# Hybrid decoder step, one core: plain products for four feed-forward pairs while the second token group's blocks are built, weight sums on DVE, and loads moved ahead

## The chip, the cores and the metric

The kernel runs on one core of a Trainium2 chip. The metric is device time in microseconds (us); lower is better. Five engines work side by side: PE (TensorE, matmuls and transposes), DVE (VectorE), ACT (ScalarE), POOL (GpSimd) and SP, which here only issues DMA transfers. Each engine goes through its own list of instructions in order; semaphores hold an instruction until what it reads is there or what it overwrites is free. PE writes to PSUM banks; everything else lies in SBUF or in device memory.

## The reference, cut to what matters

One decoder layer over 1024 prompt tokens and 32 sample tokens (1056 in all, width 1024): three branches, a gated merge, an output projection, and a gated feed-forward block (width 2816).

```python
merged = (sigmoid(g_a) * (y_a @ w_branch[:A_W]) + sigmoid(g_dn) * (y_dn @ w_branch[A_W:A_W + DN_V])
          + sigmoid(g_m) * (y_m @ w_branch[A_W + DN_V:]))
x = x + merged @ w_o
gate, up = split(rmsnorm(x, norm_ffn) @ w_up, 2)
x = x + (silu(gate) * up) @ w_down
y = rmsnorm(x, norm_final)
```

All values are 32-bit floats, and the result has to keep that precision.

## The kernel before, in words

**Three matmuls for one product.** PE multiplies in a shortened format, so each operand is split in a high and a low half (`split`: ACT casts the high half, DVE subtracts it from the source to get the low one), and a product is the sum of high*high, high*low and low*high. The tiles `pc` hold split weights, `raw` the weights as loaded, `bx` the split blocks of activations.

**Stages.** Up to about 1047 us the branches, ending with the last third of the merge (L273 to L275). Then the output projection `w_o` with the residual (`w_o_group`), the feed-forward up products with SiLU (`up_chunk`, to about 1661 us), the down products (L1246 to L1251, to about 1932 us), and the final norm.

**Token groups.** Group 0 holds the 128-token tiles 0, 2, 1, 3 and group 1 the tiles 4, 6, 5, 7 and the 32 sample tokens, called token 8. For each tile `w_o_group` makes two halves of 512 columns over eight blocks k of the inner dimension; DVE adds the residual out of PSUM (`tadd`), ACT squares and sums. After the second half `norm_t` (called once for each tile) reads the first half back from device memory, makes the factor `rstd` on DVE in twelve small steps, scales both halves of `xo` on DVE (L1206, L1207; `xo` has one buffer), PE transposes the eight blocks (L1213), and ACT writes them to `xf` with the gain (L1217). `combine` then makes differences of two tiles' blocks (on POOL for group 0, on DVE for group 1), and `put` splits each of the seven blocks 11, 21, 22, T1 to T4 into `bx`.

**Up products.** For each of 22 pairs f (128 columns of gate and 128 of up) and each group g, `up_chunk` uses the Strassen-Winograd form: seven block products of 12 matmuls each, 256 columns wide for group 0 and 272 for group 1, so 84 matmuls. The blocks of weights are seven pieces made by `up_pieces`: two DMA loads into `raw`, four sums or differences on POOL into a third `raw` tile and in place, and seven splits. Results come out of PSUM by DVE adds (L92), SiLU on ACT, two DVE products (L89), and two DMA stores to `dH`. The order `seq` is: group 0 of f = 0 to 6 (`NA` = 7), group 1 of f = 0 to 6, then both groups of f = 7 to 19 one after the other, and last (20,0), (21,0), (20,1), (21,1). Whoever changes f calls `up_pieces` anew, so it is called 31 times (62 loads). `raw` is a ring of 5 tiles and `pc` one of 8.

**Down products.** `h_load` reads `dH` back into `hr` (3 buffers) and splits it into `hx`, which lie in a pool `dp` that is opened once the up stage's pools are closed; `wd_load` loads the weights. At the end of each tile the residual is read as a whole row tile `x2` (512 KB).

**What sets the order.** A scheduler that goes by the priorities in `high_priority` (`AHEAD` = 3000, `CHAIN` = 4500) writes one list per engine. Pools decide when a load may start: a tile of a new pool waits until the tiles that lay there are done with.

Of the kernel before, what the change touches and what calls it, by code (L numbers as in the profile page):

```python
# [34 lines left out]
NA = 7  # L35
# [14 lines left out]
def kernel(  # L50
# [1101 lines left out]
    def sub_pool(name, side="left"):  # L1152
        c = ctx.enter_context(ExitStack())
        return c, c.enter_context(tc.tile_pool(name=name, bufs=1, side=side, reuse_waits="tile"))

    wctx, wp = sub_pool("wp")

    def raw_t():
        return wp.tile([P, 1024], F32, tag="raw", bufs=5, name=nm("raw"))

    def pc_t():
        return wp.tile([P, 1024], F32R, tag="pc", bufs=8, name=nm("pc"))
# [23 lines left out]
    def piece_tiles(pool_, g):  # L1186
        BX[g] = {p: pool_.tile([P, 2, 4, GN[g]], F32R, name=f"bx{g}{p}") for p in PIECES}
# [12 lines left out]
    def norm_t(i, x2, ss):  # L1200
        rows = tok[i][1]
        xo = wo.tile([P, D], F32, tag="xo", bufs=1, name=nm("xo"))
        nc.sync.dma_start(xo[:rows, 0:512], dX2[i][:rows, 0:512])
        add(V, ss[:rows, 0:1], ss[:rows, 0:1], ss[:rows, 1:2])
        r = rstd_of(ss[:rows, 0:1], 1, "rstd")
# [3 lines left out]
        for kh in range(2):  # L1209
            b = bank("d").rearrange("p (k c) -> p k c", k=4)  # L1210
            for kk in range(4):
                k = 4 * kh + kk
                T.transpose(b[:, kk, :rows], xo[:rows, k * P:(k + 1) * P], ident[:rows, :rows])  # L1213
            f = xf_t()
            for kk in range(4):
                k = 4 * kh + kk
                A.activation(f[:, kk, :rows], b[:, kk, :rows], AF.Copy, scale=gains[:, 2 * KT + k:2 * KT + k + 1])  # L1217
            out.append(f[:, :, :rows])
        return out

    def combine(g, cs, b11, b21, b12, b22):
        n = cs.stop - cs.start
        t1, t2 = (tt_t()[:, :, :n] for _ in range(2))
        E = V if g else G
        sub(E, t1, b12, b11)
        sub(E, b12, b22, b12)
        put(g, "11", cs, b11)
        put(g, "T1", cs, t1)
        sub(E, t2, b22, t1)
        put(g, "22", cs, b22)  # L1230
        put(g, "T3", cs, b12)
        put(g, "21", cs, b21)
        put(g, "T2", cs, t2)
        sub(E, b21, b21, t2)
# [20 lines left out]
    def tadd(b, i, x2, cs, lo):  # L1255
        rows = tok[i][1]
        add(V, x2[:rows, cs], b[:rows], x2[:rows, cs])
        if rows < P:
            A.copy(lo[:NS], b[NS:2 * NS])
            add(V, x2[:NS, cs], lo[:NS], x2[:NS, cs])  # L1260

    def w_o_group(g):
        ssq = {}
        for hf in range(2):
            cs = slice(hf * 512, hf * 512 + 512)
            ws = []
            for k2 in range(4):
                raw, hi, lo = raw_t(), pc_t(), pc_t()
                with tc.high_priority(offset=AHEAD):
                    nc.sync.dma_start(raw.rearrange("p (k c) -> p k c", k=2),  # L1270
                                      w_o[0, k2 * 256:(k2 + 1) * 256, cs].rearrange("(k p) c -> p k c", p=P))
                    split(hi, lo, raw)
                ws.append([a.rearrange("p (k c) -> p k c", k=2) for a in (hi, lo)])
            held = {}
            for i in groups[g]:
                t0, rows = tok[i]
                with tc.high_priority(offset=300):
                    x2 = x2_load(i, cs)
                b = bank("b")
                for k in range(KT):  # L1280
                    hi, lo = ws[k // 2]
                    x = X[k]
                    tmm(b, i, hi[:, k % 2], lo[:, k % 2], x[:, 0, t0:t0 + rows], x[:, 1, t0:t0 + rows], xs[:, k],
                        k == 0, k == KT - 1)
                pri = ExitStack()
                if hf == 1:
                    pri.enter_context(tc.high_priority(offset=CHAIN))
                tadd(b, i, x2, slice(0, 512), tt_t().rearrange("p k c -> p (k c)") if rows < P else None)
                if hf == 0:
                    ssq[i] = wo.tile([P, 2], F32, tag="ssq", bufs=5, name=nm("ssq"))  # L1290
                A.activation(bank("d")[:rows], x2[:rows], AF.Square, accum_out=ssq[i][:rows, hf:hf + 1])
                nc.sync.dma_start(dX2[i][:rows, cs], x2[:rows])
# [245 lines left out]
```

## Time and profile before

| | |
|---|---|
| time, median of 3 runs (lowest, highest) | 1943.93 us (1940.45, 1944.67) |
| the profiled execution, its own time | 1943.94 us |
| its span | 1941.8 us |
| PE busy | 1866.9 us (96%) |
| PE weight load busy | 1727.6 us (89%) |
| DVE busy | 1116.3 us (57%) |
| ACT busy | 716.2 us (37%) |
| POOL busy | 330.7 us (17%) |
| TensorE clock granted, mean of the span | 0.982 |

The span is the profiled part of one execution, and its rows are in microseconds from the span's start. A matmul's busy time is longer than the distance to the next matmul, since matmuls overlap in the array; what one costs is the stretch divided by the count, in a stretch without idle time. The granted clock (PEclk) is 1.00 at 2.4 GHz and 0.50 at 1.2 GHz; a value between them is a stretch with some of both. A wait is shown as who waited, for which instruction of which engine.

### The profile page before, as it was taken

How to read it: one execution, taken by the hardware profiler on the slowest of the kernel's cores; microseconds unless marked ns; L12 is line 12 of the kernel's file. 1: busy time of each engine (PE TensorE's matmuls, PEld its weight loads, DVE VectorE, ACT ScalarE, POOL GpSimd, SP SyncE). 2: the span in 40 equal slices, each digit the busy share in tenths (PEclk: the TensorE clock that was granted, in tenths of full speed). 3: DMA queues.
4: the chain of work that ended last, by engine and by line, in shares of the span. 5: the costliest groups of instructions: out<-in, count | busy, mean ns of one | idle time of the engine just before them, and what ended most of it. 6: DMA issues, size and time to landing. Idle time of an engine off the chain costs nothing. (4 is left out here: it accounts for less than half of the span.)

```text
span 1941.8 us, 31597 instructions
## 1 busy us (share of the span) xinstructions
PE 1866.9 (96%) x12145; PEld 1727.6 (89%) x12145; DVE 1116.3 (57%) x2558; ACT 716.2 (37%) x1539; POOL 330.7 (17%) x366
## 2 busy tenths in 40 slices
PE   6999999999999999999998998789999999899997
PEld 6799998889999999999998878789999999787776
DVE  6666477545743466622147479989665658456224
ACT  5523463234323452222222355444332324344121
POOL 3100011011000012000023044534232323001000
PEclk9999999999999999999999998889999999999999
DMA  5122123331322334321344534324232233855311
GB/s 171 33 69 80 47 67 94 110 117 58 105 83 64 90 94 125 113 72 43 109 145 173 175 117 128 115 76 121 70 92 75 67 94 123 288 185 188 110 64 46
DMA packets 229746, 203.58 MB, mean 105 GB/s; under 512 B 21284, under 2 KB 188121, under 8 KB 229596
## 3 DMA queue, kind: packets, MB, share of 16 engines
q1 hardware_dynamic: 229596, 201.58, 33.6%
q8 instruction: 95, 1.56, 0.3%
q14 instruction: 55, 0.45, 0.1%
HBM read 163.41 MB, written 38.12 MB: 104 GB/s over the span
## 5 line engine op out<-in xcount | busy, mean ns | idle before, releaser
L273 PE MATMUL psb<-x,whi 128*128 128x384 f32 (+1 forms) x1272 | 418.3, 329 | 1.6 <-ACT whi L102 1.2
L275 PE MATMUL psb<-x,wlo 128*128 128x384 f32 (+1 forms) x1272 | 415.2, 328 | 0.5 <-DVE wlo L95 0.5
L274 PE MATMUL psb<-x,whi 128*128 128x384 f32 (+1 forms) x1272 | 415.2, 327 | 0.0
L95 DVE TENSOR_TENSOR pc<-raw,pc 128x512 fp32r<-128x512 f32 (+1 forms) x278 | 273.3, 990 | 137.3 <-ACT pc L102 131.5
L102 ACT CAST pc<-raw 128x512 fp32r<-128x512 f32 (+1 forms) x278 | 196.1, 716 | 263.5 <-PE psb L1368 121.1
L273 PEld LDWEIGHTS psb<-x,whi 128*128 128x128 f32 x1272 | 239.6, 188 | 5.3 <-issue 1.9
L275 PEld LDWEIGHTS psb<-x,wlo 128*128 128x128 f32 x1272 | 239.9, 189 | 3.5 <-DVE wlo L95 1.4
L274 PEld LDWEIGHTS psb<-x,whi 128*128 128x128 f32 x1272 | 239.8, 189 | 3.1 <-issue 2.0
L1366 PE MATMUL psb<-bx,pc 128*128 128x272 f32 (+1 forms) x528 | 154.5, 293 | 9.5 <-DVE ev L92 7.4
L95 POOL TENSOR_TENSOR raw<-raw,raw 128x512 f32<-128x512 f32 x93 | 143.5, 1556 | 75.5 <-DVE pc L95 53.2
L95 DVE TENSOR_TENSOR wlo<-raw,whi 128x1024 fp32r<-128x1024 f32 x73 | 90.6, 1241 | 110.9 <-ACT whi L102 107.3
L1367 PE MATMUL psb<-bx,pc 128*128 128x272 f32 (+1 forms) x528 | 153.8, 291 | 0.0
L1368 PE MATMUL psb<-bx,pc 128*128 128x272 f32 (+1 forms) x528 | 153.2, 291 | 0.4 <-DVE rstd L110 0.4
L1246 PE MATMUL psb<-pc,hx 128*128 128x512 f32 x344 | 136.8, 398 | 6.0 <-ACT hx L102 6.0
L92 DVE TENSOR_TENSOR ev<-psb,ev 128x256 f32<-128x256 f32 (+1 forms) x220 | 93.9, 427 | 78.7 <-PE psb L1368 67.2
L1247 PE MATMUL psb<-pc,hx 128*128 128x512 f32 x344 | 137.0, 398 | 0.0
L1248 PE MATMUL psb<-pc,hx 128*128 128x512 f32 x344 | 132.4, 397 | 0.0
L1366 PEld LDWEIGHTS psb<-bx,pc 128*128 128x128 f32 x528 | 103.3, 196 | 11.0 <-ACT pc L102 5.1
L102 ACT CAST whi<-raw 128x1024 fp32r<-128x1024 f32 x73 | 76.5, 1048 | 89.3 <-PE psb L274 71.4
L1366 PE MATMUL psb<-bx0T,pc 128*128 128x256 f32 x352 | 101.0, 287 | 6.1 <-DVE ev L92 6.0
L1368 PEld LDWEIGHTS psb<-bx,pc 128*128 128x128 f32 x528 | 103.2, 196 | 0.7 <-DVE rstd L110 0.7
L1367 PEld LDWEIGHTS psb<-bx,pc 128*128 128x128 f32 x528 | 103.6, 196 | 0.1
(496 smaller groups left out, 3970.0 us busy)
## 6 DMA issues: line engine op xcount, KB each, us to landing
raw<-in_w_ffn_up_dram SPq DMA_DIRECT2D x62, 512.0 KB, 4.6
raw<-in_w_in_dram SPq DMA_DIRECT2D x56, 512.0 KB, 3.9
raw<-in_w_ffn_down_dram SPq DMA_DIRECT2D x44, 512.0 KB, 3.4
raw<-in_w_o_dram SPq DMA_DIRECT2D x16, 512.0 KB, 8.1
raw<-in_w_branch_dram SPq DMA_DIRECT2D x12, 512.0 KB, 3.8
dH<-ev SPq DMA_DIRECT2D x44, 136.0 KB, 3.4
hr<-dH SPq DMA_DIRECT2D x22, 272.0 KB, 3.1
dH<-ev SPq DMA_DIRECT2D x44, 128.0 KB, 1.7
```

Of the source, the lines that this page charges most:

```text
L92: eng.tensor_tensor(out, a, b, op=ALU.add)
L95: eng.tensor_tensor(out, a, b, op=ALU.subtract)
L102: A.copy(hi, src)
L273: T.matmul(o, w_h, xh[k][:, cs], start=k == 0, stop=False)
L274: T.matmul(o, w_h, xl[k][:, cs], start=False, stop=False)
L275: T.matmul(o, w_l, xh[k][:, cs], start=False, stop=k == nk - 1)
L1246: T.matmul(b, xh, wh, start=first, stop=False)
L1247: T.matmul(b, xh, wl, start=False, stop=False)
L1248: T.matmul(b, xl, wh, start=False, stop=last)
L1366: T.matmul(b, w[:, 0, k], x[:, 0, k], start=start and k == 0, stop=False, skip_group_check=not start)
L1367: T.matmul(b, w[:, 0, k], x[:, 1, k], start=False, stop=False, skip_group_check=not start)
L1368: T.matmul(b, w[:, 1, k], x[:, 0, k], start=False, stop=k == 3, skip_group_check=not start)
```

## The change

**Plain products.** `NA` is 4. Group 0 of f = 0 to 3 is no longer made by `up_chunk` but by `up_plain`: two loads, two splits over all 1024 columns, and eight block products of 12 matmuls (96 instead of 84) on the blocks 11, T1, 22 and 21, with four DVE adds and products and no weight sums. Group 1 of f = 0 to 3 is made by `up_chunk` later: one each is put in behind f = 6, 10, 14 and 18 (`QOUT`). `up_pieces` is called 24 times (48 loads, and 8 loads for the plain products).

**Sums and differences on DVE.** The four sums of `up_pieces` and the differences of `combine` of both groups are made by DVE.

**Norms.** `norm_pair` makes `rstd` for two tiles at once; `xo` is scaled by ACT and has two buffers. Group 1 goes through as (8), (4, 6), (5, 7), and all its `w_o` products stand ahead of the up products.

**Pools.** `raw` and `pc` lie in two pools, the first of them there while the merge still runs, and `raw` has 4 tiles. The first two `w_o` loads of the first half (k = 0 to 3) are issued and split during the merge. `ev` has 8 + 8 buffers used in turn. A pool `hp` with 11 `hx` and the 3 `hr` is opened where the blocks of group 0 lay. The down stage's residual comes by halves (`xl`, 2 buffers, 256 KB). `norm_final`'s gain is loaded early in the up stage.

```diff
-NA = 7
+NA = 4
+QOUT = 4
...
+    wps = [sub_pool("wpa")[1]]
...
+    def raw_t():
+        return ring_t("raw", 4, 2, F32)
+
+    def pc_t():
+        return ring_t("pc", 8, 4, F32R)
...
+        if f2 >= 2:
+            w_o_pre.append(w_o_load(0, f2 - 2))
...
-    def raw_t():
-        return wp.tile([P, 1024], F32, tag="raw", bufs=5, name=nm("raw"))
...
-    def norm_t(i, x2, ss):
...
-        V.tensor_scalar(xo[:rows, 0:512], xo[:rows, 0:512], r[:rows], None, op0=ALU.mult)
-        V.tensor_scalar(xo[:rows, 512:], x2[:rows], r[:rows], None, op0=ALU.mult)
...
+    def norm_pair(pair, x2s, ssq):
...
+        with tc.high_priority(offset=CHAIN):
+            r = rstd_of(ss[:rows, :n], n, "rstd")
...
+            xo = wo.tile([P, D], F32, tag="xo", bufs=2, name=nm("xo"))
+            nc.sync.dma_start(xo[:rows, 0:512], dX2[i][:rows, 0:512])
+            A.activation(xo[:rows, 512:], x2s[i][:rows], AF.Copy, scale=r[:rows, j:j + 1])
+            A.activation(xo[:rows, 0:512], xo[:rows, 0:512], AF.Copy, scale=r[:rows, j:j + 1])
...
-        E = V if g else G
-        sub(E, t1, b12, b11)
-        sub(E, b12, b22, b12)
+        sub(V, t1, b12, b11)
...
+    for pair, out in w_o_group(1, ((8,), (4, 6), (5, 7))):
+        todo.append((pair, out))
...
+    def up_plain(f):
...
+            for c0 in (f * P, DFF + f * P):
                 raw, hi, lo = raw_t(), pc_t(), pc_t()
+                nc.sync.dma_start(raw.rearrange("p (k c) -> p k c", k=KT), w_ffn_up[0, :, c0:c0 + P].rearrange("(k p) c -> p k c", p=P))
+                split(hi, lo, raw)
...
+            prod(b1, w, 0, "11", True, True)
+            p1_, c2 = ev_t(256), ev_t(256)
+            A.copy(p1_, b1)
+            prod(b2, w, 0, "T1", True, False)
+            prod(b2, w, 4, "22", False, True)
+            add(V, c2, b2, p1_)
+            prod(b1, w, 4, "21", False, True)
...
-            add(G, s1, a21, a22)
-            sub(G, s2, s1, a11)
+            add(V, s1, a21, a22)
+            sub(V, s2, s1, a11)
             piece("11", a11)
-            sub(G, s3, a11, a21)
+            sub(V, s3, a11, a21)
...
-            sub(G, s4, a12, s2)
+            sub(V, s4, a12, s2)
             piece("S4", s4)
...
-    seq = [(f, g) for g in range(2) for f in range(NA)]
+    for f in range(NA):
+        up_plain(f)
...
     for f in range(NA, NF - 2):
         seq += [(f, 0), (f, 1)]
+        if late_b and (f - NA) % QOUT == 2:
+            seq.append((late_b.pop(0), 1))
...
+    hp = sub_pool("hp")[1]
     bctx.close()
-
     dctx, dp = sub_pool("dp")
...
-        raw = dp.tile([P, 544], F32, tag="hr", bufs=3, name=nm("hr"))[:, :n]
-        hx = dp.tile([P, 2, 544], F32R, tag="hx", bufs=24, name=nm("hx"))[:, :, :n]
+        raw = hp.tile([P, 544], F32, tag="hr", bufs=3, name=nm("hr"))[:, :n]
+        hx = hx_t()[:, :, :n]
...
-                    with tc.high_priority(offset=100):
-                        nc.sync.dma_start(x2[i][:rows], dX2[i][:rows])
...
+                xl = dp.tile([P, 512], F32, tag="xl", bufs=2, name=nm("xl"))
+                with tc.high_priority(offset=60):
+                    nc.sync.dma_start(xl[:rows], dX2[i][:rows, cs])
```

The lists of the engines show the change at three places. A row has the line, the operation, what is written and read, and the shape.

PE before, at the last transposes of group 1 (`xo` of tile 7, then of token 8), between the last product of group 0 of f = 6 and the first of group 1 of f = 0:

```order
L1368 MATMUL psb_1804_12799<-bx022_11058,pc_1800_12793 128x256
L1213 MATMUL psd_1643_11783<-ident_69,xo_1639_11763 128x128 x4
L1213 MATMUL psd_1645_11793<-ident_69,xo_1639_11763 128x128 x4
L1213 MATMUL psd_1655_11849<-ident_69,xo_1651_11829 128x32 x4
L1213 MATMUL psd_1657_11859<-ident_69,xo_1651_11829 128x32 x4
L1366 MATMUL psb_1822_12933<-bx111_11873,pc_1815_12910 128x272
L1367 MATMUL psb_1822_12933<-bx111_11873,pc_1815_12910 128x272
```

PE after, at the first transposes of the pair (5, 7), inside the plain products of f = 3:

```order
L1364 MATMUL psb_1709_12286<-bx021_10825,pc_1704_12275 128x256 x2
L1247 MATMUL psd_1643_11773<-ident_69,xo_1642_11769 128x128 x4
L1247 MATMUL psd_1645_11783<-ident_69,xo_1642_11769 128x128 x4
L1364 MATMUL psb_1709_12286<-bx021_10825,pc_1705_12276 128x256
L1364 MATMUL psb_1713_12340<-bx011_10824,pc_1707_12281 128x256 x2
L1364 MATMUL psb_1713_12340<-bx011_10824,pc_1708_12282 128x256
```

Between the last transposes and the first product that reads group 1 stood nothing; now the products of f = 3 that remain and those of (4,0) stand there, and token 8 comes first of its group instead of last.

DVE before, in the group 1 passes over f = 0 to 6 (`pc` is a split of a weight piece, `ev` a result out of PSUM):

```order
L95 TENSOR_TENSOR pc_13051<-raw_13044,pc_13051 128x512
L92 TENSOR_TENSOR ev_12963<-psb_12934,ev_12949 128x272
L95 TENSOR_TENSOR pc_13054<-raw_13042,pc_13054 128x512
L92 TENSOR_TENSOR ev_12977<-psb_12935,ev_12963 128x272
L92 TENSOR_TENSOR ev_12991<-psb_12936,ev_12977 128x272
L95 TENSOR_TENSOR pc_13057<-raw_13044,pc_13057 128x512
L95 TENSOR_TENSOR pc_13060<-raw_13040,pc_13060 128x512
```

DVE after, in the passes over both groups (`raw` is a sum or difference of weights):

```order
L93 TENSOR_TENSOR raw_13766<-raw_13764 128x512
L96 TENSOR_TENSOR raw_13766<-raw_13766,raw_13762 128x512
L96 TENSOR_TENSOR raw_13764<-raw_13762,raw_13764 128x512
L93 TENSOR_TENSOR ev_13592<-psb_13550,ev_13578 128x256
L96 TENSOR_TENSOR raw_13762<-raw_13762,raw_13766 128x512
L93 TENSOR_TENSOR ev_13606<-psb_13551,ev_13592 128x256
L93 TENSOR_TENSOR ev_13634<-psb_13550,ev_13578 128x256
L90 TENSOR_TENSOR ev_13620<-ev_13620,ev_13634 128x256
L93 TENSOR_TENSOR ev_13649<-psb_13551,ev_13578 128x256
L96 TENSOR_TENSOR pc_13773<-raw_13766,pc_13773 128x512
```

The four weight sums of the next f now stand in DVE's list between the results of the running one, ahead of the splits; before they had a list of their own on POOL.

SP before, at the end of the up stage (`dH` stores of the last pair, and the first loads of `hr`, `y` being the residual):

```order
L1396 DMA dH_10790<-ev_17547 128x272
L1444 DMA raw_17872<-in_w_ffn_down_dram 128x2x512
L1397 DMA dH_10790<-ev_17576 128x272
L1433 DMA hr_17638<-dH_10771 128x512
L1433 DMA hr_17655<-dH_10772 128x512
L1433 DMA hr_17678<-dH_10773 128x512
L1444 DMA raw_17912<-in_w_ffn_down_dram 128x2x512
L1417 DMA g_fin<-in_norm_final_dram 128x1024
L1444 DMA raw_17928<-in_w_ffn_down_dram 128x2x512
L1490 DMA y_17978<-dX_0_10760 128x1024
```

SP after, in front of the last two `dH` stores:

```order
L1506 DMA hr_17599<-dH_10793 128x512
L1517 DMA raw_17426<-in_w_ffn_down_dram 128x2x512
L1455 DMA dH_10804<-ev_17233 128x272
L1517 DMA raw_17536<-in_w_ffn_down_dram 128x2x512
L1506 DMA hr_17622<-dH_10794 128x512
L1506 DMA hr_17639<-dH_10795 128x512
L1456 DMA dH_10804<-ev_17262 128x272
L1517 DMA raw_17616<-in_w_ffn_down_dram 128x2x512
L1506 DMA hr_17662<-dH_10796 128x512
L1517 DMA raw_17576<-in_w_ffn_down_dram 128x2x512
L1506 DMA hr_17679<-dH_10797 128x512
L1455 DMA dH_10805<-ev_17370 128x272
```

Before, the first `hr` load came after the last `dH` store; now most of the first pass's `hr` loads stand ahead of it, between the stores.

## Rows read from the trace of the kernel before

**Rows 1.** The page, part 1: busy us (share of the span) and instructions.

```profile
span 1941.8 us, 31597 instructions
PE 1866.9 (96%) x12145; PEld 1727.6 (89%) x12145; DVE 1116.3 (57%) x2558; ACT 716.2 (37%) x1539; POOL 330.7 (17%) x366
```

**Rows 2.** Stretches: length; busy (count) PE, PEld, DVE, ACT, POOL; PEclk; DMA share; GB/s.

```profile
1040.00:1060.00 20.00, 13.42 (x68) 12.00 (x67) 16.28 (x29) 7.86 (x13) 0.71 (x3) 0.83 0.14 49
...
1160.00:1260.00 100.00, 84.67 (x608) 81.31 (x606) 97.62 (x177) 49.89 (x115) 50.33 (x33) 0.88 0.39 117
1260.00:1280.00 20.00, 9.78 (x59) 9.28 (x58) 11.97 (x39) 9.59 (x33) 0.72 (x1) 0.59 0.10 30
1280.00:1340.00 60.00, 60.00 (x481) 59.99 (x480) 57.82 (x77) 28.44 (x56) 34.34 (x23) 1.00 0.38 113
1340.00:1640.00 300.00, 300.00 (x2449) 299.87 (x2449) 190.81 (x320) 100.65 (x203) 96.43 (x65) 1.00 0.29 87
...
1660.00:1680.00 20.00, 15.28 (x57) 11.93 (x56) 8.68 (x12) 7.15 (x11) 0.00 (x0) 0.83 0.92 313
1680.00:1700.00 20.00, 18.70 (x81) 14.82 (x80) 8.90 (x12) 8.96 (x13) 0.00 (x0) 1.00 0.86 304
1720.00:1920.00 200.00, 200.00 (x861) 155.59 (x860) 74.82 (x133) 55.35 (x80) 7.49 (x21) 1.00 0.33 110
1920.00:1942.00 22.00, 12.02 (x52) 9.37 (x50) 16.09 (x74) 2.90 (x8) 0.00 (x0) 0.84 0.28 101
```

**Rows 3.** PE's waits from 1040 us on: total us, times, longest.

```profile
PE psb L1366 <- DVE ev L92: 13.4, 8, 3.7
PE psd L1213 <- DVE xo L1206: 10.4, 3, 8.9
PE psb L1246 <- ACT pc L102: 6.6, 1, 6.6
PE psb L1246 <- ACT hx L102: 6.0, 2, 4.7
```

**Rows 4.** PE in order of time: start, us, operation [idle before, releaser]; token 8's transposes.

```profile
1269.18 1.03 PE L1213 MATMUL psd<-ident,xo 32*128 32x32 f32 x8 [8.89 <-DVE xo L1206]
```

**Rows 5.** DVE's groups by form, 1160 to 1280 us: count, busy us, mean ns.

```profile
L95 DVE TENSOR_TENSOR pc<-raw,pc 128x512 fp32r<-128x512 f32 x57 | 50.9, 907 | 2.5 <-ACT pc L102 2.5
L92 DVE TENSOR_TENSOR ev<-psb,ev 128x256 f32<-128x256 f32 x35 | 14.4, 412 | 0.0
L98 DVE SCALAR_TENSOR_TENSOR rstd<-rstd,rstd 128x1 f32<-128x1 f32 x24 | 11.9, 495 | 0.0
...
L95 DVE TENSOR_TENSOR tt<-xf,xf 128x512 f32<-128x512 f32 x2 | 1.4, 692 | 1.1 <-ACT xf L1217 1.1
...
L98 DVE SCALAR_TENSOR_TENSOR rstd<-rstd,rstd 32x1 f32<-32x1 f32 x6 | 0.9, 147 | 0.2
```

**Rows 6.** DVE in order of time, 1300 to 1310 us: start, us, operation.

```profile
1301.59 0.68 DVE L95 TENSOR_TENSOR pc<-raw,pc 128x512 fp32r<-128x512 f32 x1
1302.19 0.43 DVE L92 TENSOR_TENSOR ev<-psb,ev 128x272 f32<-128x272 f32 x1
1302.54 2.56 DVE L95 TENSOR_TENSOR pc<-raw,pc 128x512 fp32r<-128x512 f32 x2
```

**Rows 7.** POOL in order of time, 1300 to 1310 us.

```profile
1303.26 1.29 POOL L92 TENSOR_TENSOR raw<-raw 128x512 f32<-128x512 f32 x1 [3.44 <-DVE pc L95]
```

**Rows 8.** DVE's groups by form, 1655 to 1700 us.

```profile
L95 DVE TENSOR_TENSOR pc<-raw,pc 128x1024 fp32r<-128x1024 f32 x9 | 10.9, 1225 | 7.3 <-ACT pc L102 3.8 <-DMA hr<-dH 2.0 <-PE psb L1368 1.5
L95 DVE TENSOR_TENSOR hx<-hr,hx 128x512 fp32r<-128x512 f32 x13 | 8.7, 690 | 16.1 <-ACT hx L102 16.1
```

**Rows 9.** SP's issues in order of time, 1652 to 1672 us.

```profile
1662.20 1.39 SPq L1433 DMA_DIRECT2D hr<-dH  x3
```

**Rows 10.** The page, part 6: DMA issues, count, KB each, median us to landing.

```profile
raw<-in_w_ffn_up_dram SPq DMA_DIRECT2D x62, 512.0 KB, 4.6
...
raw<-in_w_o_dram SPq DMA_DIRECT2D x16, 512.0 KB, 8.1
```

More of the change, by code (lines that the diff above doesn't have):

```diff
@@ L1265, in w_o_group @@
             cs = slice(hf * 512, hf * 512 + 512)
+            ws = [w_o_pre.pop(0) if w_o_pre else w_o_load(hf, k2) for k2 in range(4)]
+            for pair in pairs:
+                x2s = {}
+                for i in pair:
+                    t0, rows = tok[i]
+                    with tc.high_priority(offset=300):
+                        x2 = x2_load(i, cs)
+                    b = bank("b")
+                    for k in range(KT):
+                        hi, lo = ws[k // 2]
+                        x = X[k]
+                        tmm(b, i, hi[:, k % 2], lo[:, k % 2], x[:, 0, t0:t0 + rows], x[:, 1, t0:t0 + rows], xs[:, k],
+                            k == 0, k == KT - 1)
+                    pri = ExitStack()
+                    if hf == 1:
+                        pri.enter_context(tc.high_priority(offset=2 * CHAIN))
+                    tadd(b, i, x2, x2, tt_t().rearrange("p k c -> p (k c)") if rows < P else None)
+                    if hf == 0:
+                        ssq[i] = wo.tile([P, 2], F32, tag="ssq", bufs=5, name=nm("ssq"))
+                    A.activation(bank("d")[:rows], x2[:rows], AF.Square, accum_out=ssq[i][:rows, hf:hf + 1])
+                    nc.sync.dma_start(dX2[i][:rows, cs], x2[:rows])
+                    x2s[i] = x2
+                    pri.close()
+                if hf == 1:
+                    with tc.high_priority(offset=CHAIN):
+                        out = norm_pair(pair, x2s, ssq)
+                    yield pair, out
@@ new lines, in build_pair @@
+    def build_pair(g, pair, out):
+        with tc.high_priority(offset=CHAIN):
+            if pair[0] < 8:
+                c = (pair[0] - 4 * g) * P
+                lo_, hi_ = out
+                combine(g, slice(c, c + P), lo_[0], lo_[1], hi_[0], hi_[1])
+            else:
+                s0, s1 = out[0]
+                combine(g, slice(256, 272), s0[:, :, :16], s1[:, :, :16], s0[:, :, 16:], s1[:, :, 16:])
+    piece_tiles(xa, 0)
+    for pair, out in w_o_group(0, ((0, 2), (1, 3))):
+        build_pair(0, pair, out)
@@ L1266, in w_o_group @@
+    todo = []
+    for pair, out in w_o_group(1, ((8,), (4, 6), (5, 7))):
+        todo.append((pair, out))
+    xctx.close()
+    g_fin = sub_pool("gf", "right")[1].tile([P, D], F32, name="g_fin")
+    bctx, xb = sub_pool("xb", "right")
+    piece_tiles(xb, 1)
+    for pair, out in todo:
+        build_pair(1, pair, out)
+    octx.close()
+    def up_plain(f):
+        with tc.high_priority(offset=AHEAD):
             ws = []
-            for k2 in range(4):
+            for c0 in (f * P, DFF + f * P):
@@ L1268, in w_o_group @@
                 raw, hi, lo = raw_t(), pc_t(), pc_t()
[L1269 to L1292, printed above, removed]
-                if hf == 1:
-                    held[i] = norm_t(i, x2, ssq[i])
-                pri.close()
-                if hf == 1:
-                    yield i, held
@@ new lines, in prod @@
+        def prod(b, w, k0, x, start, stop):
+            x = BX[0][x]
+            for k in range(4):
+                for wi, xi in ((0, 0), (0, 1), (1, 0)):
+                    T.matmul(b, w[wi][:, k0 + k], x[:, xi, k], start=start and k == wi == xi == 0, stop=stop and k == 3 and wi == 1,
+                             skip_group_check=True)
+        res = []
+        for w in ws:
+            b1, b2 = (bank("b")[:, :256] for _ in range(2))
+            prod(b1, w, 0, "11", True, True)
[5 more added lines that the diff above has]
+            prod(b1, w, 4, "21", False, True)
+            res.append((b1, c2))
@@ L1397, in up_chunk @@
         nc.sync.dma_start(dH[f][:, c0 + n:c0 + 2 * n], c12)
[L1399 removed]
+    for f in range(NA):
+        up_plain(f)
+    ectx, ev1 = sub_pool("ev1")
+    evs.append(ev1)
+    nev[0] = 0
+    seq = []
+    late_b = list(range(NA))
     for f in range(NA, NF - 2):
         seq += [(f, 0), (f, 1)]
+        if late_b and (f - NA) % QOUT == 2:
+            seq.append((late_b.pop(0), 1))
     seq += [(NF - 2, 0), (NF - 1, 0), (NF - 2, 1), (NF - 1, 1)]
+    assert not late_b
     prev, W = None, None
[L1404 to L1405 removed]
+    for f, g in seq:
         if f != prev:
```

135 lines of the change are left out of this document (72 added, 63 removed).

## The prediction, made before the changed kernel ran

> **What bounds the kernel now.** I read the page's busy times first: PE is busy for 96% of the span and DVE for 57% [rows 1]. That is an average over stages, so the stretches come next [rows 2]. They show a PE that runs without a gap in most of them and loses time in three. To price a loss I need what one matmul costs where nothing is lost. From 1720 to 1920 us, 861 matmuls of 512 columns take 200 us: 0.2323 us each. From 1280 to 1340 us 481 matmuls of 272 columns take 60 us: 0.1247. From 1340 to 1640 us 2449, half of 256 and half of 272 columns, take 300 us: 0.1225, so 256 columns cost 0.1203.
>
> Losses by these prices, all [rows 2 and 3]:
> - 1040 to 1060 us: PE waits 6.6 us for the first split of w_o (ACT pc), and the granted clock is 0.83, that is 6.8 of the 20 us at 1.2 GHz, much of it in the wait. I add 2 us for matmuls done at that level: 8.6, between 6.6 and 10.
> - 1160 to 1280 us: 608 + 59 matmuls at 0.1203 are 80.2 us of work in 120: 39.8 lost. PE waits there for DVE: 13.4 us for its results out of PSUM, 10.4 for the scaling of xo, the longest 8.9 ahead of token 8's transposes [rows 4]. The rest, some 16 us, is matmuls at 1.2 GHz: PEclk is 0.88 and then 0.59. DVE is the engine that is late, 97.6 of 100 us busy.
> - 1660 to 1700 us: 57 + 81 matmuls at 0.2323 are 32.1 us in 40: 7.9 lost. PE waits 6.0 us for hx, since the first load of hr is issued at 1662.20 [rows 9], and PEclk is 0.83 in the first half.
>
> Together 56.3 us. The tail behind 1920 us (12 us of PE work in 22) is the last tiles' norm and stores, and stays.
>
> **The change part by part.**
>
> *Added matmuls.* Four f times 96 - 84 are 48 matmuls of 256 columns: 48 x 0.1203 = **+5.8 us**, all on the path, as PE is the bound. With all three losses gone the span would be 1941.8 - 56.3 + 5.8 = 1891.3 us.
>
> *Start of w_o.* The order has 36 matmuls that read the two early loads (k = 0 to 3 of three tiles) ahead of the first that needs the other two. They are 36 x 0.2323 = 8.4 us of cover, and the wait that they replace was 6.6. A w_o load lands 8.1 us after its issue at the median [rows 10] and is split in about 2 us, but the later two are issued while the merge still runs. I take 0 left, between 0 and 6.6 (the cover gone).
>
> *The plain stage.* From the first plain product to the first that reads a T2 of group 1, PE has 384 x 0.1203 = 46.2 us of plain products, 40 transposes (each cheaper than a matmul of 256 columns, 4.5 us together), and 72 Strassen matmuls of (4,0), 8.7 us: 59 us. DVE's list for the same stretch has 101 instructions: 8 splits of 1024 columns at 1.225 [rows 8], 9.8 us; 36 of 512 columns (splits, differences, blocks, residual adds, the first sums) at 0.69 [rows 5], 24.8; 17 results of 256 columns at 0.42, 7.1; and 40 small ones (rstd steps at 0.15, the pieces for token 8 at about 0.2), 6.5. That is 48 us in 59, where before it was 97.6 in 100. The scaling of xo goes to ACT, 10 halves of about 0.65 each, which is 49.9 of 100 us busy there [rows 2]. So DVE is no longer the bound on average. What is late next is the chain of the last pair (5, 7): residual add, squares, twelve rstd steps, xo, transposes, differences, blocks; by the order and these durations its T2 is ready within a microsecond of when PE wants it. I leave 2.5 us lost; the ends are 0 and 12.9, which is what token 8's episode cost (1260 to 1280 us: 20 - 59 x 0.1203, [rows 2]).
>
> *Weight sums on DVE.* 4 x 0.69 = 2.8 us more DVE work in each of 24 calls. For both groups of an f DVE then has 7 splits (4.8), the sums (2.8) and 14 results at 0.43 [rows 6] (6.0): 13.6 us, against 84 x (0.1203 + 0.1247) = 20.6 of PE. In a late group 1 pass alone it is 10.6 against 10.5; the neighbours lend 7 us each. I take 0 lost in the up stage, between 0 and 4 (a microsecond at each of the four passes).
>
> This counts on the splits becoming faster once POOL is silent. The rows show it: a split alone takes 0.68 us, two beside a POOL sum of 1.29 us 2.56 together [rows 6 and 7], and the mean from 1160 to 1280 is 0.907 against 0.69 for the same form alone [rows 5]. The small rstd steps take 0.495 against 0.147 in the same way [rows 5]. If the slowness were DVE's own, a single pass would have today's 57.82 of 60 us [rows 2], 10.1 in 10.5, plus 2.8: 12.9, which is 2.4 late at each of four passes, and with matmuls at 1.2 GHz behind each wait, as in the stage before, 10 to 15 us.
> The Trainium skill (GPSIMD Engine Reference, section Architecture) says that GpSimd's ports into SBUF are shared with the vector engine; the trace agrees, 0.68 us alone and 1.28 beside POOL, and by that rule those 10 to 15 us fall away.
>
> *Up to down.* hr and 11 hx now lie where group 0's blocks were, and the loads stand in front of the last stores of dH. The 6.0 us wait should go. What is late next is DVE: in (20,1) and (21,1), 2 x 84 x 0.1247 = 21 us of PE, it has the pieces of 21 (7.6), 14 results (6.0), 11 splits of hx at 0.69 (7.6) and 6 of w_down at 1.225 (7.4) [rows 8]: 28.6. Of the 7.6 us too much most belongs to later down products, so it need not hold PE. Queued behind a waiting hr load on SP are w_down loads and dH stores, whose ev tiles have 16 buffers. I take 3 us lost, between 0 and today's 7.9. The residual's halves, issued just before their adds, ride under 200 us of down matmuls at a DMA share of 0.33: 0.
>
> *Sum.* 1891.3 + 2.5 + 3 = 1896.8 us of span. The profiled execution lies 2.1 us above its span (1943.94 to 1941.8) and at the median of the runs, 1943.93. So **1899 us**. Its own bounds: 1891.3 + 2.1, less 1.4 if the start's loss was 10, give 1892 below; above, half of the ends that can add up (6.6, 12.9, 4, 7.9) gives about 1909.
>
> **The rivals.**
> - *A, DVE's chain is still late in the plain stage.* For it: the last pair is just in time, all four engines take part in its chain, and a wait once begun drops the clock (0.59 behind token 8). Against it: 11 us of spare DVE time and transposes that are spread among products. One episode like token 8's instead of 2.5 gives 1899 - 2.5 + 12.9 = 1909; with a second and the up-to-down wait as today, 1909 + 12.9 - 3 + 7.9 = 1927. I put it at 1913. The case of slow DVE sums (above) would land in the same place, 1909 to 1914.
> - *B, slower than before: the weight sums stop DVE in each f.* With four raw tiles and three used by each call, the load of the second half needs the tile that the last piece S4 of the f before frees; the sums wait for it in DVE's list, the results of the running products stand behind them, PE's banks stay full. From that split the load (4.6 us), two sums (1.4) and the split of S2 (1.3) need 7.3 us; a single pass leaves 10.5, a double one 20. It decides where the load lands later than 8 us in a single pass and 18 in a double one; w_o's 8.1 [rows 10] shows the first to be possible. In the stage of 1160 to 1280 us 24 us of waits cost 39.8, 1.6 for each. 24 calls that wait 1.3 us each cost 24 x 1.3 x 1.6 = 50: about 1949. Against it: double passes leave far more than the load takes.
> - *C, the plain stage gains nothing*, since the order built by priorities lets the same transposes wait as before. Then only the two ends gain: 1941.8 - 8.6 - 4.9 + 5.8 + 2.1 = 1936. Against it: the order shows products behind every group of transposes.
>
> **How the numbers follow.** Forecast (1892 to 1906) 0.60; A, with the case of slow sums, 0.29; C 0.05, of which 0.02 comes out within 0.2% of before; B 0.04, of which 0.01 within; below 1892 0.02. A measurement of this kernel can tell about 0.2%, 4 us, from no change. Faster 0.94, same 0.03, slower 0.03. The range from 1890 to 1918 holds the forecast's cases and most of A's.
>
> **What would show it.** Right: no wait for ACT pc at the start of w_o; PE lists over 95 us of work per 100 in the plain stage with PEclk near 1.00; splits of 512 columns at 0.69 and no POOL rows in the up stage; up passes without a gap at about 13.6 us of DVE per 20.6; at most one short wait for hx. Wrong: PE waiting for bx of group 1 or for ev in the plain stage at PEclk under 0.9 (A), DVE waiting for DMA raw in each f (B), the waits for xo as before (C).

## The result, and the profile after

The changed kernel takes 1891.6 us at the median of four runs (1890.58 to 1893.17); the kernel before took 1943.82 beside it. The ratio is 0.9735, with a 95% interval of 0.9718 to 0.9752: 52 us or 2.65% faster. The forecast was 1899 us with a range from 1890 to 1918, so the direction and most of the size were right, and the time came out near the lower end.

The page of the changed kernel, part 1, and its clock in 40 slices, answering to [rows 1]:

```profile
span 1889.4 us, 31322 instructions
PE 1851.5 (98%) x12193; PEld 1719.1 (91%) x12193; DVE 1060.4 (56%) x2543; ACT 707.1 (37%) x1520; POOL 133.0 (7%) x234
...
PEclk9999999999999999999999999999999999999999
```

Stretches of the changed kernel, in the columns of [rows 2]. The stages lie earlier than before: w_o begins at 1045 us, the plain stage at about 1146, down at about 1610:

```profile
1040.00:1060.00 20.00, 20.00 (x98) 17.12 (x97) 13.25 (x25) 6.24 (x12) 0.71 (x3) 1.00 0.39 126
...
1160.00:1260.00 100.00, 100.00 (x827) 100.00 (x826) 69.72 (x140) 50.77 (x120) 0.00 (x0) 1.00 0.27 82
...
1260.00:1600.00 340.00, 340.00 (x2771) 340.00 (x2770) 232.14 (x446) 118.27 (x241) 0.00 (x0) 1.00 0.31 93
1600.00:1620.00 20.00, 16.59 (x105) 14.89 (x104) 16.04 (x28) 11.36 (x18) 0.00 (x0) 1.00 0.93 315
1620.00:1640.00 20.00, 20.00 (x88) 16.09 (x87) 11.80 (x15) 9.79 (x15) 0.00 (x0) 1.00 0.82 269
```

The stretch from 1160 to 1260 us had 608 PE instructions and DVE 97.62 us busy [rows 2]; it now has 827, DVE at 69.72 and the clock at 1.00. Apart from the tail, the only stretch behind 1040 us in which PE is not always busy is the one where up goes over into down. PE's waits there are all that is left of the 36 us of waits in [rows 3] (PE's waits from 1030 us on, same columns):

```profile
PE psb L1280 <- ACT pc L103: 1.8, 1, 1.8
PE psb L1425 <- DVE ev L93: 1.6, 1, 1.6
```

From here on, **lost** means this sum over PE's rows in order of time: the distance from one matmul's start to the next one's, less the distance that a matmul of that width has where nothing is late (0.120 us at 256 columns, 0.1255 at 272, 0.2325 at 512, 0.109 for a transpose). It takes in waits and the clock at once.

| lost, us | start of w_o | plain stage (before: 1140 to 1290 us) | up | up to down |
|---|---|---|---|---|
| before | 8.6 | 42.5 | 0 | 8.8 |
| changed | 0.1 | 0 | 0 | 4.2 |
| changed, second profile | 0.1 | 0 | 0 | 5.1 |

That is 55.6 us less lost, and 5.8 us more of matmuls. The span became 52.4 us shorter; of the other 2.6 us, 2.2 lie ahead of w_o, where the merge's last matmul starts at 1047.34 before and at 1045.10 after. That is no more than profiles differ there: in two of the kernels below whose code ahead of w_o is as before it starts at 1046.54 and 1044.89 us, and in the second profile of the changed kernel at 1044.47.

### The profile page after: what moved, and what is told of

Same layout as the page of the kernel before. It is cut to its first block, busy times and chain, and to the rows that moved or that the text cites. A ratio compares the mean times of both kernels' runs of the same rounds, so it can differ in the third digit from the quotient of the medians.

```text
span 1889.4 us, 31322 instructions
## 1 busy us (share of the span) xinstructions
PE 1851.5 (98%) x12193; PEld 1719.1 (91%) x12193; DVE 1060.4 (56%) x2543; ACT 707.1 (37%) x1520; POOL 133.0 (7%) x234
## 3 DMA queue, kind: packets, MB, share of 16 engines
q8 instruction: 95, 1.56, 0.4%
## 4 chain that ended last, share of the span: by engine, by line
PE 93%; DVE 2%; DMA 2%; ACT 1%; issue 1%; SPq 0%; DVEq 0%; ACTq 0%
PE psb L274 14%; PE psb L275 13%; PE psb L276 13%; PE psb L1427 7%; PE psb L1425 7%; PE psb L1426 7%; PE psb L1281 6%; PE psb L1280 6%; PE psb L1282 6%; PE psb L1364 2%; DMA x<-in_x_prompt_dram 1%; PE psa L926 1%; PE psb L1284 1%; PE psb L1285 1%; PE psa L906 1%
## 5 line engine op out<-in xcount | busy, mean ns | idle before, releaser
L96 DVE TENSOR_TENSOR pc<-raw,pc 128x512 fp32r<-128x512 f32 (+1 forms) x237 | 198.0, 845 | 155.8 <-ACT pc L103 153.8
L103 ACT CAST pc<-raw 128x512 fp32r<-128x512 f32 (+1 forms) x237 | 174.0, 745 | 260.6 <-PE psb L1281 115.2
L1426 PE MATMUL psb<-bx,pc 128*128 128x272 f32 (+1 forms) x480 | 136.4, 285 | 0.0
L1427 PE MATMUL psb<-bx,pc 128*128 128x272 f32 (+1 forms) x480 | 136.3, 286 | 0.0
L1425 PE MATMUL psb<-bx,pc 128*128 128x272 f32 (+1 forms) x480 | 135.9, 286 | 0.0
L93 DVE TENSOR_TENSOR ev<-psb,ev 128x272 f32<-128x272 f32 (+1 forms) x208 | 89.5, 431 | 63.1 <-PE psb L1427 46.7
L1425 PE MATMUL psb<-bx1T,pc 128*128 128x272 f32 x352 | 101.4, 288 | 1.6 <-DVE ev L93 1.6
L1427 PE MATMUL psb<-bx1T,pc 128*128 128x272 f32 x352 | 101.1, 288 | 0.0
L1426 PE MATMUL psb<-bx1T,pc 128*128 128x272 f32 x352 | 100.9, 287 | 0.0
L1426 PEld LDWEIGHTS psb<-bx,pc 128*128 128x128 f32 x480 | 91.0, 190 | 0.0
L1427 PEld LDWEIGHTS psb<-bx,pc 128*128 128x128 f32 x480 | 90.7, 189 | 0.0
```

Source lines behind the costliest of these rows:

```text
L93: eng.tensor_tensor(out, a, b, op=ALU.add)
L96: eng.tensor_tensor(out, a, b, op=ALU.subtract)
L103: A.copy(hi, src)
L1425: T.matmul(b, w[:, 0, k], x[:, 0, k], start=start and k == 0, stop=False, skip_group_check=not start)
L1426: T.matmul(b, w[:, 0, k], x[:, 1, k], start=False, stop=False, skip_group_check=not start)
L1427: T.matmul(b, w[:, 1, k], x[:, 0, k], start=False, stop=k == 3, skip_group_check=not start)
```

## The experiments

All are compared with the kernel before on the same chip; the changed kernel was run a second time beside one group of them and gave 0.9739 [0.9724, 0.9755]. Differences from the changed kernel are taken from the ratios (against 0.9737, times 1942 us) and read together with the lost time in the traces, since each ratio is uncertain by 1.5 thousandths, 3 us.

> The changed kernel once more, beside the three that follow, so that differences of a few microseconds are read on one chip: 0.9735 of the kernel before, PE losing 4 us between 1040 us and the tail.

### The plain products undone

```diff
     for f in range(NA):
-        up_plain(f)
+        up_chunk(f, 0, up_pieces(f))
```

> The changed kernel with the first four group 0 passes made in the Strassen form instead of plain products; their weight sums on DVE. Theory 1 (what cured the stage is that plain products need few splits): PE has 48 matmuls less, 5.8 us, but DVE gets 4 x 10.6 us of splits, sums and results in place of 4 x 4.1, about 74 us of work in a stage of 54 us of PE work: 20 us late, less 5.8, and more where the clock falls: 1905 to 1920 us, with PE waiting for DVE. Theory 2 (the norms on ACT, the order of group 1 and a silent POOL would have been enough): 1886 us.

Measured: 0.9852 [0.9837, 0.9867], 22 us slower than the changed kernel. The plain stage loses 25.4 us, which with 5.8 us fewer matmuls is 20 net. In the four stretches of this kernel where it happens (columns of [rows 2]) DVE is well loaded and the clock falls:

```profile
1160.00:1180.00 20.00, 17.66 (x120) 17.16 (x121) 18.06 (x54) 12.02 (x36) 0.00 (x0) 0.83 0.36 110
1180.00:1200.00 20.00, 16.57 (x133) 15.72 (x132) 15.69 (x33) 14.66 (x37) 0.00 (x0) 0.99 0.56 167
1200.00:1220.00 20.00, 15.28 (x99) 14.21 (x98) 17.19 (x46) 10.08 (x23) 0.00 (x0) 0.83 0.25 73
1220.00:1240.00 20.00, 17.97 (x111) 17.13 (x112) 11.39 (x20) 10.93 (x29) 0.00 (x0) 0.74 0.02 7
```

Theory 1 holds, with a reservation: DVE is not full here (62 of 80 us), and PE's waits are short and spread over several releasers (ACT pc, DVE ev, ACT xo, ACT xf), none above 2.3 us. The waits point to the chain through both engines more than to the sum of DVE's work; no run tells the two apart. Of the 42.5 us lost before, 17 are gone here too, by the other parts of the change.

### The plain products alone, put into the kernel before

```diff
-NA = 7
+NA = 4
...
-    seq = [(f, g) for g in range(2) for f in range(NA)]
+    for f in range(NA):
+        up_plain(f)
+    seq = [(f, 1) for f in range(NA)]
```

> The kernel before with the plain products alone: group 0 of f = 0 to 3 plain, then group 1 of f = 0 to 3, then both groups of f = 4 to 19 as before; sums on POOL, norms, pools and order of group 1 as before. Theory 1 (plain passes take the load off DVE): the stage's DVE work falls to about its PE work, some 46 against 50 us, the loss of 40 us falls to 10 to 20, less 5.8 for the added matmuls: 1918 to 1930 us. Theory 2 (without the norms on ACT and the new order the transposes wait anyway, with fewer passes to cover them): the loss stays, 1945 us or more.

Measured: 0.9932 [0.9914, 0.9951], 13 us faster than before. The stage's loss falls from 42.5 to 20.2 us, less the 5.8 of added matmuls. What is left is one kind of wait (PE's waits from 1140 to 1290 us):

```profile
PE psd L1213 <- DVE xo L1206: 14.6, 3, 8.9
PE psb L1401 <- ACT bx L1191: 1.3, 1, 1.3
```

The 13.4 us of waits for DVE results [rows 3] are gone, and the wait of 8.9 for token 8's xo is there as before. So the plain products cure the results, and the norms of group 1 are a second trouble of their own.

### The weight sums on DVE alone, in the kernel before

```diff
-            add(G, s1, a21, a22)
-            sub(G, s2, s1, a11)
+            add(V, s1, a21, a22)
+            sub(V, s2, s1, a11)
```

(and the two others in the same way)

> The kernel before with one part of the change alone: the four weight sums of each pair on DVE instead of POOL. Theory 1 (DVE is full in the stage from 1160 to 1280 us because of the Strassen passes' splits, and the sums add 7 x 2.8 = 19 us there, while about 28 us of slowness beside POOL fall away): a small gain, PE still loses 25 to 35 us there, 1930 to 1942 us. Theory 2 (contention with POOL is the cause): the loss falls under 10 us, 1910 us or less.

Measured: 0.9978 [0.9968, 0.9987], 4 us faster. POOL is nearly silent (5.93 us busy from 1140 to 1290, against 64.32 before), and yet the stage loses 36.6 us. PE goes without a gap until 1220 us and then stands:

```profile
1200.00:1220.00 20.00, 20.00 (x169) 20.00 (x168) 18.67 (x46) 9.97 (x20) 0.00 (x0) 1.00 0.46 133
1220.00:1240.00 20.00, 9.23 (x78) 9.03 (x77) 19.09 (x40) 10.07 (x25) 0.00 (x0) 0.81 0.51 152
1240.00:1260.00 20.00, 3.88 (x16) 3.14 (x16) 13.20 (x43) 9.93 (x29) 0.00 (x0) 0.50 0.05 17
```

```profile
PE psd L1213 <- DVE xo L1206: 30.0, 3, 14.9
```

The waits for results became waits for xo: 30.0 us in place of 10.4 [rows 3]. The longest, 14.9, falls in a stretch where DVE is 19.09 of 20 us busy and the steps of rstd stand between splits and sums; the other two, 6.2 and 8.9, come when DVE has time (13.20 of 20 us). Theory 2 falls: contention with POOL alone was not what made the stage late. Theory 1 has the time right (1936.8 us) and a full DVE, with more lost than its 25 to 35 us.

### The weight sums back on POOL, in the changed kernel

The reverse of the diff above.

> The changed kernel with one part undone: the four weight sums of each Strassen pair are made by POOL again, all else as changed. Theory 1 (the plain products took the load off DVE, and the sums have slack wherever they run): the splits of 512 columns go back from 0.69 us to a mean near 0.9, DVE's busy time from 1260 to 1600 us stays near 230 us, and PE still loses nothing in the up stage and 0 to 3 us in the plain stage, where only the pieces of f = 4 and 5 are made: 1891 to 1895 us. Theory 2 (the contention of POOL with DVE is what made DVE late before, and moving the sums is what cured it): PE waits for DVE results in the plain stage and behind the single passes, 10 us and more: 1901 us or later.

Measured: 0.9788 [0.9774, 0.9803], 10 us slower. The plain stage loses 0.8 us and the passes up to 1590 us 0.5, as theory 1 has it, so the cure there does not hang on where the sums are made. But 10.0 us are lost at the end of up, where the changed kernel loses 4 to 5; neither theory had that. Also wrong: DVE does not stay near 230 us from 1260 to 1600 us but falls to 196.94, and its splits take 0.760 us on the mean, not 0.9. POOL's list at the end of up points to the reason (start, us, operation, [idle before, releaser]):

```profile
1585.57 1.29 POOL L93 TENSOR_TENSOR raw<-raw 128x512 f32<-128x512 f32 x1 [7.46 <-DMA raw<-in_w_ffn_up_dram]
1586.93 4.24 POOL L96 TENSOR_TENSOR raw<-raw,raw 128x512 f32<-128x512 f32 x3
1600.27 1.30 POOL L93 TENSOR_TENSOR raw<-raw 128x512 f32<-128x512 f32 x1 [9.10 <-DMA hr<-dH]
1601.65 5.06 POOL L96 TENSOR_TENSOR raw<-raw,raw 128x512 f32<-128x512 f32 x3
```

In the changed kernel the same four sums are on DVE (the last call but one of `up_pieces`, DVE in order of time):

```profile
1582.20 0.69 DVE L93 TENSOR_TENSOR raw<-raw 128x512 f32<-128x512 f32 x1 [0.76 <-DMA raw<-in_w_ffn_up_dram]
1583.14 1.28 DVE L96 TENSOR_TENSOR raw<-raw,raw 128x512 f32<-128x512 f32 x2
1584.68 0.68 DVE L96 TENSOR_TENSOR raw<-raw,raw 128x512 f32<-128x512 f32 x1
```

From the first sum's start to the last one's end it is 5.6 to 6.4 us on POOL, and 3.0 to 4.4 on DVE with what stands between them. The next load waits for a tile that these pieces free: the last weight load of the up stage is issued at 1594.23 us with POOL's sums and at 1588.73 in the changed kernel. At the end four single passes of 10.5 us stand in a row, and there the delay reaches PE, which waits for ACT pc, DVE pc and DVE ev between 1599 and 1616 us. In the passes over both groups, and in the lone group 1 passes between them, it does not. That the chain of sums is the cause is read from these rows; the longest wait, 2.8 us for DVE ev up to 1616 us, also has loads of `hr` and of w_down behind it.

### Both undone at once

> The changed kernel with both undone at once: the first four group 0 passes in the Strassen form and all weight sums on POOL. Strassen alone cost about 21 us against the changed kernel, POOL sums alone about 9 to 10, nearly all of it at the end of the up stage. Theory 1 (in the plain stage the two act together: DVE is full there, and what makes each split slower makes PE late): more than the sum of both, 1925 us or later. Theory 2 (DVE's instruction count is what matters, and sums on POOL take 4 x 2.8 us off it): less than the sum, 1912 to 1918 us.

Measured: 0.9904 [0.9889, 0.9919], 32 us slower; Strassen alone cost 22 and POOL sums alone 10. The sum is met, and neither theory: in the plain stage 29.5 us are lost instead of 25.4, so the two act together there by 4 us at most, and 10.5 are lost at the end of up, against 5.6 with Strassen alone.

### One weight pool, opened after the merge

```diff
-    wps = [sub_pool("wpa")[1]]
+    wps = []
...
-        return ring_t("raw", 4, 2, F32)
+        return ring_t("raw", 4, 4, F32)
...
-        if f2 >= 2:
-            w_o_pre.append(w_o_load(0, f2 - 2))
```

(`pc` in the same way, both pools' tiles in the one opened behind the merge, and the first yD back in its pool)

> The changed kernel with the weight tiles in one pool that is opened only when the merge's pools are closed, as before the change (4 raw, 8 pc), and no early w_o loads. ACT's list then has the casts of the w_o weights behind the last casts of the merge again. Theory 1: the wait of 6.6 us in front of w_o is that of these casts, not of the loads, and it comes back with the 1.2 GHz stretch: 8.6 us, 1900 us. Theory 2 (other parts of the change cover the start of w_o): 1892 us.

Measured: 0.9776 [0.9762, 0.9791], 8 us slower, with 8.2 us lost at the start of w_o: theory 1. First PE, then ACT of this kernel in order of time:

```profile
1051.88 2.07 PE L1278 MATMUL psb<-pc,x 128*128 128x512 f32 x4 [5.79 <-ACT pc L103]
```

```profile
1050.45 0.43 ACT L103 CAST x<-sgD 128x288 fp32r<-128x288 f32 x1 [0.42 <-DVE sgD L93]
1050.79 3.88 ACT L103 CAST pc<-raw 128x1024 fp32r<-128x1024 f32 x4
```

SP issues the w_o loads at 1022.84 us here, so the data is there long before. The four casts wait in ACT's list behind the last cast of the merge, which comes 4 us after PE's last merge matmul. In the changed kernel the first two w_o loads are cast at 952 us, long before that tail.

### hr and hx in one late pool

```diff
-    hp = sub_pool("hp")[1]
...
-        p_, b_ = (hp, 11) if (nhx[0] - 1) % 24 < 11 else (dp, 13)
-        return p_.tile([P, 2, 544], F32R, tag="hx", bufs=b_, name=nm("hx"))
+        return dp.tile([P, 2, 544], F32R, tag="hx", bufs=24, name=nm("hx"))
```

(`hr` in `dp` in the same way)

> The changed kernel with hr and all hx in the pool dp again, so that the first hr load stands behind the last dH store. Theory 1 (the place of hr and hx decides the start of down): PE waits for hx about 6 us and the clock falls: the loss there goes from 3.7 to 8 or 9 us, so 1896 us. Theory 2 (DVE's work at the end of the up stage decides, whatever the place): the loss stays near 4 us, 1892 us.

Measured: 0.9764 [0.9748, 0.9780], 5 us slower; 8.5 us lost against 4.2 and 5.1. The first hr load is issued at 1614.13 us, right behind the last dH store, and PE's wait is the old one [rows 3]:

```profile
PE psb L1280 <- ACT hx L103: 5.3, 1, 5.3
```

Theory 1 holds; the place is worth 3 to 5 us, about half of the 8.5 that are lost without it.

### xo on DVE, three plain pairs, and two tries at the last wait

```diff
-            A.activation(xo[:rows, 512:], x2s[i][:rows], AF.Copy, scale=r[:rows, j:j + 1])
+            V.tensor_scalar(xo[:rows, 512:], x2s[i][:rows], r[:rows, j:j + 1], None, op0=ALU.mult)
```

(and the other half)

> The changed kernel with xo scaled by DVE again (two halves for each tile at 0.47 us), still in pairs and with two xo buffers. Theory 1 (DVE has 11 us to spare in the plain stage, so 8 halves, 3.8 us, are covered; the waits for xo before came from one buffer and a full DVE): within 2 us of the changed kernel. Theory 2 (the scaling on DVE itself held the transposes): PE waits for xo as before, 5 to 10 us more.

Measured: 0.9749 [0.9734, 0.9763]. The profiled execution has a span of 1890.0 against 1889.5 beside it, loses 0 us in the plain stage and shows no wait of PE for xo. It is the fastest of four, though; the median lies 2.9 us above that of the changed kernel beside it, which is inside the uncertainty. So theory 2 falls: the scaling on DVE does not hold the transposes any more. Theory 1's 2 us are not settled.

`NA = 3` in place of 4:

> The changed kernel with three plain pairs instead of four: 12 matmuls less, 1.4 us, and 11.6 us less PE work in front of the first product that reads group 1. In the changed kernel T2 of group 1 was ready 3 us before PE read it. Theory 1 (the chain of the last pair (5, 7) sets when the blocks are ready): PE comes 11.6 us sooner and the blocks some 4 us, as DVE has 4.1 us less to do: a wait of 4 to 8 us, 1.6 times that with the clock, less 1.4: 5 to 11 us slower than the changed kernel. Theory 2 (DVE's load sets it, and with less load the blocks keep ahead): 1.4 us faster.

Measured: 0.9747 [0.9729, 0.9765], 2 us slower than the changed kernel and inside the uncertainty. Neither theory: 2.0 us are lost in the plain stage, but in front of transposes (PE waits 2.1 us for ACT xo of the pair (4, 6)), not for the blocks. Counted from the first plain product (1146.59 us here, 1145.69 with four pairs), the blocks' last T split starts 3.8 us sooner, as theory 1 had it. PE reads T2 first at 1199.3, 6.5 us sooner by the same count: the scheduler wove the first products of group 1 with what was left of group 0, and so put off the need by some 3 us (11.6 sooner and 2.1 of wait would have been 9.5). A difference between three and four plain pairs is not shown.

A fourth hr buffer (`bufs=4`):

> The changed kernel with four hr buffers instead of three (and 24 small sample tiles instead of 26, for the space). In the changed kernel three hr loads hold SP's queue from 1593 to 1599 us, since each waits for a buffer, and the w_down load behind them comes at 1600.3; PE then waits twice, 1.6 and 1.8 us. Theory 1 (the hr ring holds up w_down on SP): w_down comes sooner and 2 to 3 of the 3.7 us at the start of down go. Theory 2 (DVE's own work there is too much for the time): no difference above 1 us.

Measured: 0.9746 [0.9731, 0.9760], 5.7 us lost instead of 4 to 5: theory 2.

A raw tile of its own for the first w_down load:

```diff
-        raw, hi, lo = raw_t(), pc_t(), pc_t()
+        nwd[0] += 1
+        raw = hp.tile([P, 1024], F32, tag="wr", bufs=1, name=nm("raw")) if nwd[0] % 5 == 1 else raw_t()
+        hi, lo = pc_t(), pc_t()
```

> The changed kernel with one more tile for loaded weights in the down stage only: every fifth w_down load, the first among them, goes into a tile of its own in the pool hp (10 instead of 11 hx there, one xl, 22 small sample tiles). In the changed kernel the first w_down load, at 1600.3 us, waits for a raw tile in SP's queue, the hr load behind it lands at 1604.6, and ACT stands still for it for 2.9 us with the last results and casts behind it. Theory 1 (the ring of four raw tiles holds SP there): ACT's wait and PE's two waits shrink, 2 to 3 us less. Theory 2 (DVE and ACT have too much work at the end of the up stage): within 1 us of the changed kernel.

Measured: 0.9735 [0.9721, 0.9750], span 1889.0, 3.4 us lost: within 1 us of the changed kernel, theory 2. ACT's wait for hr did not go, it moved forward, and a wait for w_down came behind it (ACT in order of time, 1596 to 1614 us):

```profile
1598.09 0.62 ACT L103 CAST hx<-hr 128x512 fp32r<-128x512 f32 x1 [7.29 <-DMA hr<-dH]
1607.55 0.62 ACT L103 CAST hx<-hr 128x512 fp32r<-128x512 f32 x1 [0.59 <-DMA hr<-dH]
1611.41 1.05 ACT L103 CAST pc<-raw 128x1024 fp32r<-128x1024 f32 x1 [3.24 <-DMA raw<-in_w_ffn_down_dram]
```

What holds the last 4 us is not settled: neither ring alone does. No version ran clearly faster than the changed kernel. Undone one by one, the plain products, the sums, the early weight pool and the place of `hr` and `hx` cost 22, 10, 8 and 5 us; the norms but for xo's engine, the 16 `ev` buffers, the order of the late group 1 passes and the residual by halves were not undone by themselves.

## Why the prediction was right, and where its sizes were off

**The bound and the three losses: right.** PE was the bound, and nearly all that was gained lies in the three stretches named. The sum came out 7.4 us too high, and the steps that make this up are these:

- *The losses before*, 56.3 us by the rows' counts, are 59.9 by start-to-start distances: 42.5 in place of 39.8 in the plain stage, since all 667 instructions of the stretch were priced as matmuls though some were cheaper transposes and the stretch was cut at 1160 us; and 8.8 in place of 7.9 at the start of down. 3.6 us.
- *The plain stage*, 2.5 us left by the forecast, lost nothing: another 2.5. "Within a microsecond of when PE wants it" was off by little; DVE's last T2 split begins at 1201.19 us and takes 0.68, and PE reads T2 from 1204.9, 3.0 us later:

```profile
1201.19 0.68 DVE L96 TENSOR_TENSOR bx1T<-tt,bx1T 128x512 fp32r<-128x512 f32 x1
1201.80 0.42 DVE L93 TENSOR_TENSOR ev<-psb,ev 128x256 f32<-128x256 f32 x1
1202.13 0.68 DVE L96 TENSOR_TENSOR bx1T<-xf,bx1T 128x512 fp32r<-128x512 f32 x1
```

- *The part ahead of w_o*, put at no change, is 2.2 us shorter. That is within what profiles differ there (1044.89 to 1047.34 us with the code as before), so it is luck as far as the runs show.
- *Up to down*, put at 3 us, lost 4.2 and 5.1: 1.2 to 2.1 the other way. The 0.4 us that remain are less than the prices of the matmuls can tell.

**Added matmuls: right.** PE has 48 instructions more (x12193 against x12145), and no stretch of the up stage shows a gap.

**Start of w_o: right, with the cause of the old wait left out.** The 8.6 us went, and came back as 8.2 when the pools were undone. The cover was as forecast: PE's 36 matmuls on the two early loads run from 1045.23 to 1053.63 us, and ACT casts the other two loads from 1051.57 us on, with about 1 us to spare. But the step had only a load's 8.1 us to landing for what might be late. The loads had been issued at 1025 us before; the casts, from 1053.13 us on, stood behind the merge's in ACT's list. The early pool helps because it lets ACT cast in front of the merge's tail.

**Plain stage: right in its main point.** Undone, the plain products cost 22 us; alone, they gain 13. The step counted DVE's work against PE's, 48 in 59 us and 101 instructions; from the first plain product to the first T2 read DVE has 44.18 us in 59.21, in 106. But it took DVE's load for the whole cause of the old loss, though its rows held token 8's wait. The kernel before with the plain products shows that the norms of group 1, with one xo buffer and token 8 last, are a loss of their own: 14.6 us of waits for xo, most of them while DVE is 15.44 of 20 us busy (1200 to 1220 us). Which of the norms' parts cures it (pairs, two buffers, token 8 first) was not tried one by one; that the scaling on ACT is not needed for it, the run with xo on DVE shows.

**Weight sums: right that they cost nothing in the up stage, with too much weight on contention.** DVE has 232.14 us of work from 1260 to 1600 us; times 20.6 / 340 that is 14.1 us for both groups of an f, where 13.6 was forecast. The forms answer to [rows 5] and [rows 6] (DVE by form in that stretch):

```profile
L96 DVE TENSOR_TENSOR pc<-raw,pc 128x512 fp32r<-128x512 f32 x136 | 92.4, 690 | 28.2 <-ACT pc L103 26.7
L96 DVE TENSOR_TENSOR raw<-raw,raw 128x512 f32<-128x512 f32 x60 | 39.5, 685 | 0.5
L93 DVE TENSOR_TENSOR ev<-psb,ev 128x272 f32<-128x272 f32 x88 | 38.7, 440 | 9.4 <-issue 2.6 <-PE psb L1427 2.4
...
L93 DVE TENSOR_TENSOR raw<-raw 128x512 f32<-128x512 f32 x20 | 13.9, 693 | 21.0 <-DMA raw<-in_w_ffn_up_dram 21.0
```

The splits are at 0.690 and the sums at 0.685, as priced. The case that the slowness beside POOL were DVE's own is out. What the Trainium skill says of the shared ports (GPSIMD Engine Reference, section Architecture) agrees with the trace once more: with POOL's sums back the same splits take 0.760 us on the mean. What slow splits would have cost with the sums on DVE, the step's 10 to 15 us, no run shows. DVE has less to do with the sums on POOL, contention and all, 196.94 us against 232.14. What the move brings, 10 us by the times and 8 by the spans of the profiles, it brings for the most part at the end of up (10.0 us lost there against 4.2 and 5.1), by the rows above as a shorter way from a load to the pieces. The prediction had no such term.

**Rivals.** *A*, a late chain in the plain stage, did not come about. *B*, DVE stopped by loads in each f, is there in small: DVE waits 21.0 us for w_ffn_up from 1260 to 1600 us, 1.0 for each of the 20 calls (the last row above), with 6 us of slack behind it. *C* did not come about, though the kernel with DVE sums alone, at 1937 us, looks just like it: the transposes wait as before.

**Up to down: the right size, and only half the reason.** One of the two waits is for DVE ev, as forecast; behind it stands ACT, idle 2.9 us for an hr load with results and casts queued behind that cast (changed kernel, ACT in order of time):

```profile
1605.59 0.62 ACT L103 CAST hx<-hr 128x512 fp32r<-128x512 f32 x1 [2.87 <-DMA hr<-dH]
1606.12 0.42 ACT L1452 ACTIVATE ev<-ev 128x272 f32<-128x272 f32 x1
1606.45 1.03 ACT L103 CAST pc<-raw 128x1024 fp32r<-128x1024 f32 x1
```

## What to carry to other kernels

Where an engine beside the bound is full in one stage, look there for work that can be made in a form with less preparation: 12 more matmuls for each pair cost 1.45 us and, by the operations' durations, took some 6.5 us off DVE (against Strassen pieces with their sums on DVE). Such a stage can hold two troubles in a row, and curing the first alone shows only the second (4 us gained from the sums alone, 13 from the plain products alone, some 37 in this stage from all parts together, 42.5 less the added matmuls); so undo the parts from the finished kernel as well as adding them to the old one. When a short operation is moved to another engine, compare the length of its chain from a load to its user, not the engines' busy times alone.

## What the runs showed of the hardware

A POOL difference of 128x512 took 1.56 us on the mean from 1280 to 1620 us in the kernel before, where DVE's splits of that size took 0.931, and 1.34 from 1260 to 1600 us in the changed kernel with the sums back on POOL, where the splits took 0.760. In these two kernels both engines' instructions are slower together or faster together; what sets how much was not tried. In the kernel before and the variants that still lose much in the plain stage, PE's waits there cost more than their length: in the kernel before with DVE sums, 31.3 us of waits for xo and bx lost 36.6, with the granted clock at 0.50 (1.2 GHz) from 1240 to 1260 us, behind a stretch in which PE did 78 matmuls and transposes in 20 us. With three plain pairs a single wait of 2.1 us lost 2.0. With waits of 1.6 and 1.8 us, at the start of down in the changed kernel, the clock stayed at 1.00 (2.4 GHz) in that profile; with 2.3 and 0.6 us, in the second one, it was 0.91 there.
